# Full-height score products, and GpSimd taken off SBUF arithmetic from the output projection on

## The chip, the cores and the metric

The kernel is one launch on one core of a Trainium2 chip. The core has a matrix engine (TensorE, PE in the profile; its weight loads are listed apart as PEld), a vector engine (VectorE, DVE), a scalar engine (ScalarE, ACT), GpSimd (POOL) and SyncE (SP), which here issues most of the DMA transfers. The metric is the device time of one execution in microseconds. Before the change the median of three runs is 1672.14 us (1669.34 to 1674.14).

## The reference

One layer of a hybrid decoder, for a prompt of 1024 tokens and for 8 sequences with 4 new tokens each, 1056 columns in all, all in float32. Cut to what matters here:

```
h = rmsnorm(x) * (1 + scale1) + shift1;   z = h @ w_in + b_in      # q, k, v, forget gate, GLU, two gates
prompt:  s = q k^T / 8 + C_i - C_j, masked;  o = softmax(s) v      # 8 heads of 64, 1024 x 1024
sample:  the same against a paged cache of 1024 keys
y_b = depthwise convolution, layernorm, silu, @ w_pb + b_pb;  y_a = o @ w_pa
m = sigmoid(gate_a) * y_a + sigmoid(gate_b) * y_b
x = x + g1 * (m @ w_o)                                             # output projection, 1024 x 1024
h2 = rmsnorm(x) * (1 + scale2) + shift2
x = x + g2 * ((silu(h2 @ Wg) * (h2 @ Wu)) @ w_ffn_out)             # feed-forward, 2816 hidden
y = rmsnorm(x)
```

## The kernel before, in words

Activations lie with channels on the 128 partitions and tokens along the free axis. To come near float32 with the fast matrix format, each operand is split in a high part (a rounded copy, made on ScalarE) and a low part (operand minus high part, made on VectorE or GpSimd), and a product is three products: high times high, high times low, low times high.

The stages, in order: modulation vectors (`ada`), input projection, values, decode attention, the convolution branch (`glu`), and from about 410 us the prompt attention, with the gates' projections and the rest of `ada` filling in. Then the two branch projections (`branch`), the output projection with `w_o` (L1068 to L1092, in three column blocks c of 352 tokens), the feed-forward's first half (`hidden`, 22 tiles t), and its second half (`out`).

**Prompt attention.** A unit is a head h and a pair of query blocks c2; `softmax_rows` makes one block's scores in chunks of up to 512 keys. For each chunk TensorE runs two products into one PSUM tile: L813 over all 128 rows, and L816. The tile `q` of a head holds q's high part (negated) in one half of the partitions and the low part in the other, `k` holds the high part of k in both halves, so L813 gives high times high plus low times high. `kl` holds the low part of k in one half, and L816 takes only those 64 rows: high times low. On a diagonal chunk a third product, L815, adds the mask between them. There are 96 chunks. VectorE adds the forget term and finds the minimum (L818), ScalarE takes the exponential (L824), VectorE or ScalarE scales (L829, L827), TensorE transposes (L871), ScalarE and VectorE split the result (L873, L874), and TensorE multiplies by v (L883, L884). Two units are kept waiting between scores and `weighted`. `load_head` (L834) fetches a head's tiles about one head ahead.

**Feed-forward.** The first half runs products over blocks with a seven-product scheme: `pair_weights` (L1128) reads two weight tiles, forms sums and differences of their halves and splits seven operands (`split`, L1120); `half_factors` (L993) does the same for the activations of one half q of the tokens (`modulated` L1004, `split_u` L1018, sums L1030 to L1040). Half 0 is prepared while `w_o` still works on the last block, half 1 after tile t = 2 has begun; tiles 0 to 3 run first for half 0 alone, and for half 1 at the end.

**The order of the work.** The program is written in one order, and a list scheduler with a time model of its own places instructions on each engine; `high_priority` moves a piece ahead. Each engine then works its own list strictly in that order, so an instruction that waits holds all that stand behind it. From `w_o` on GpSimd carries: the weight split for every second tile of the last `w_o` block (L1074 to L315), L1030 and L1033 and the `split_u` of two operands in `half_factors`, and the four sums of `pair_weights` for t = 1, 2, 3 when one half alone runs.

Of the kernel before, what the change touches and what calls it, by code (L numbers as in the profile page):

```python
# [9 lines left out]
F32 = mybir.dt.float32  # L10
# [3 lines left out]
OP = mybir.AluOpType  # L14
# [15 lines left out]
KD = D // P  # L30
# [57 lines left out]
def hybrid_step(ctx, tc, xT, cT, vec, bvf, con, stT, ptab, ptabr, kcT, vc, lfc, w_ada, w_in, w_vfa, w_vfb,  # L88
                w_pa, w_pb, w_o, w_fi, w_fo, yT, kT, vO, vsO, lfO, ucp, ucs):
    nc = tc.nc  # L90
    pe, act, dve, pool, sp = nc.tensor, nc.scalar, nc.vector, nc.gpsimd, nc.sync
# [323 lines left out]
    for i, w in enumerate(first):  # L415
        ps = ps_mm()
# [4 lines left out]
        b = sm.tile([P, 1], F32, name="bsh", tag="bsh", bufs=4)  # L421
# [118 lines left out]
    for half, (src, w0, nw) in enumerate(((w_vfa, 0, 256), (w_vfb, 256, 264))):  # L540
# [261 lines left out]

    def softmax_rows(h, i, t, ck, q, k, kl):

        sl = slice(64 * (h % 2), 64 * (h % 2) + 64)
        n = P * (i + 1)
        m = sm.tile([P, 4], F32, name="mx", tag="mx", bufs=6)
        prev = 3e38
        qb = slice(i * P, (i + 1) * P)
        for nm, s0 in enumerate(range(0, n, 512)):  # L810
            w = min(512, n - s0)
            ps = ps_s()
            pe.matmul(ps[:, :w], q[:, qb], k[:, s0:s0 + w], start=True, stop=False)  # L813
            if s0 + w == n:
                pe.matmul(ps[:, w - P:w], identr, maskr, start=False, stop=False)  # L815
            pe.matmul(ps[:, :w], q[sl, qb], kl[sl, s0:s0 + w], start=False, stop=True)  # L816

            dve.tensor_tensor_reduce(out=t[:, s0:s0 + w], in0=ps[:, :w], in1=ck[:, s0:s0 + w], scale=1.0, scalar=prev,  # L818
                                     op0=OP.add, op1=OP.min, accum_out=m[:, nm:nm + 1])
            prev = m[:, nm:nm + 1]  # L820
        cq = Cq[:, i, h:h + 1]
        st = sm.tile([P, 4], F32, name="st", tag="st", bufs=6)
        dve.scalar_tensor_tensor(st[:, 1:2], prev, cq, cq, op0=OP.subtract, op1=OP.add)
        act.activation(t[:, :n], t[:, :n], AF.Exp, bias=st[:, 1:2], scale=-1.0, accum_out=st[:, 2:3])  # L824
        dve.reciprocal(st[:, 3:4], st[:, 2:3])
# [8 lines left out]
    def load_head(h):  # L834

        p, h2 = divmod(h, 2)
        qd, kd = qkD[p]
        sl = slice(64 * h2, 64 * h2 + 64)

        def head_tile(name, dt=F32R):  # L840
            return atl.tile([P, NP], dt, name=name, tag=f"{name}{h2}", bufs=1)

        q, k, kl = head_tile("q2"), head_tile("k2"), head_tile("kl")
        ck, vh = head_tile("ck", F32), head_tile("vh").rearrange("p (b n) -> p b n", n=P)
        for r in range(2):
            sp.dma_start(q[64 * r:64 * r + 64, :].bitcast(F32), qd[r ^ h2][sl, :])
            sp.dma_start(k[64 * r:64 * r + 64, :].bitcast(F32), kd[0][sl, :])
        sp.dma_start(kl[sl, :].bitcast(F32), kd[1][sl, :])
        sp.dma_start(ck, cD[h:h + 1, :].broadcast_to([P, NP]))
        sp.dma_start(vh.bitcast(F32), vD[p][:, :, h2, :])  # L850
        heads[h] = (q, k, kl, ck, vh)
# [141 lines left out]
    def half_factors(q, new):  # L993

        o = q * SUP
        if q:
            ms = ev(uq, "ms", 1, (P, KD, DB, DT))
            msf = ms.rearrange("p k b t -> p k (b t)")
            for k in range(KD):
                dve.tensor_tensor(msf[:, k, :], X(k)[:, NP:], R[:, NP:], OP.mult)  # L1000
            dve.tensor_tensor(ms, ms, gS[:, 1, :, :].unsqueeze(3).broadcast_to([P, KD, DB, DT]), OP.mult)
            dve.tensor_tensor(ms, ms, mod[:, 24:24 + KD, 1:9].unsqueeze(3).broadcast_to([P, KD, DB, DT]), OP.add)

        def modulated(i, half):  # L1004
# [12 lines left out]

        def split_u(b, k, u, eng=dve):  # L1018
            act.copy(b[0][:, k, :], u[:, k, :])
            eng.tensor_tensor(b[1][:, k, :], u[:, k, :], b[0][:, k, :].bitcast(F32), OP.subtract)  # L1020

        ks = [slice(KS * k, KS * k + KS) for k in range(4 // KS)]
        u11, u21, u12, u22 = [modulated(i, half) for half in range(2) for i in range(2)]
        b11, b21, t1, t2, b22, t3, t4 = bs = new()
        for k in ks:
            split_u(b11, k, u11)
        for k in ks:
            split_u(b21, k, u21)
        for k in ks:
            pool.tensor_tensor(u11[:, k, :], u12[:, k, :], u11[:, k, :], OP.subtract)  # L1030
            split_u(t1, k, u11)
        for k in ks:
            pool.tensor_tensor(u12[:, k, :], u22[:, k, :], u12[:, k, :], OP.subtract)  # L1033
            split_u(b22, k, u22, pool)
            dve.tensor_tensor(u22[:, k, :], u22[:, k, :], u11[:, k, :], OP.subtract)
            split_u(t2, k, u22)
        for k in ks:
            split_u(t3, k, u12, pool)
        for k in ks:
            dve.tensor_tensor(u21[:, k, :], u21[:, k, :], u22[:, k, :], OP.subtract)  # L1040
            split_u(t4, k, u21)
        return bs
# [25 lines left out]
    for c in range(3):  # L1068
        o = CW3 * c
        s = sm.tile([P, 400], F32, name="s1", tag="ssum", bufs=2)  # L1070
        for j in range(KD):

            where = () if c == 0 and j < 2 else (lt2, ("wh3", "wl3"), 3)
            w = split_ahead(w_o[j], KD, pool if c == 2 and j % 2 else dve, *where)  # L1074
            xr = ev(lt2, "xr", 3)
            for ch, (co, cn) in enumerate(CH):
                lo, hi = max(o, co), min(o + CW3, co + cn)
                if lo < hi:
                    at = KD * co + j * cn - co
# [45 lines left out]
        dve.tensor_tensor(w[:, 1, :n], raw, w[:, 0, :n].bitcast(F32), OP.subtract)  # L1125
        return w

    def pair_weights(t, eng):  # L1128

        g, u = [raw_tile(w_fi[r * HT + t], KD * P) for r in range(2)]  # L1130
        a11, a12, a21, a22 = g[:, :512], g[:, 512:], u[:, :512], u[:, 512:]
        ws = [split(a11), split(a12)]
        s1 = ev(fb or uq, "s1", 2 if fb else 1, (P, 512))
        eng.tensor_tensor(s1, a21, a22, OP.add)  # L1134
        ws.append(split(s1))
        eng.tensor_tensor(a21, a11, a21, OP.subtract)
# [262 lines left out]
```

## Time and profile before

| | |
|---|---|
| median of 3 runs | 1672.14 us |
| profiled execution | 1673.01 us, span 1671.2 us from first to last instruction |
| PE busy (matmul) | 1600.6 us, 96% |
| PEld busy (weight load) | 1486.8 us, 89% |
| DVE busy | 1074.1 us, 64% |
| ACT busy | 702.6 us, 42% |
| POOL busy | 251.9 us, 15% |
| mean granted TensorE clock | 0.980 of full speed |

The span and the execution's own time differ by 1.8 us, spent before the first and after the last instruction. TensorE is the engine that is nearly always occupied, but a busy matmul record includes the time in which it waits inside the engine; whether the weight loads run without gaps tells more. The mean share hides the stages: PEld is at its full share in most of them and lower in the prompt attention and in a stretch around 900 to 1000 us, and these two are what the tables of stretches are to be read for.

### The profile page before, as it was taken

The page shows a single profiled execution, that of the slowest core. Times are in us where ns is not written, and L with a number is a line of the kernel's source. Part 1 is how long each engine was busy: PE and PEld are TensorE (multiplying, and loading weights), DVE is VectorE, ACT ScalarE, POOL GpSimd, SP SyncE. Part 2 cuts the span into 40 slices and gives each one's busy share as a digit, 9 for nine tenths or more (in the row PEclk, how much of TensorE's full clock was granted, in tenths as well). Part 3 has the DMA queues.
Part 4 walks back from the last instruction along what each step waited for, and adds up shares of the span by engine and source line. Part 5 has one row for each costly group of instructions (what it writes and reads, how often), then busy time and mean ns, then how long its engine had stood idle before and what let it go on. Part 6 is the DMA issues. An engine that isn't in the chain of part 4 may idle for free.

```text
span 1671.2 us, 29144 instructions
## 1 busy us (share of the span) xinstructions
PE 1600.6 (96%) x10988; PEld 1486.8 (89%) x10988; DVE 1074.1 (64%) x2119; ACT 702.6 (42%) x1395; POOL 251.9 (15%) x185
## 2 busy tenths in 40 slices
PE   6999999999999999999999789999999999999997
PEld 4999978788867777989998779999999999999997
DVE  6943389999787757234678995555555587324654
ACT  4552212122476555434554554333333365324442
POOL 2121113332220001125305430000000030000000
PEclk9999999999999979999999899999999999999998
DMA  9186576877486654354674322222222246424552
GB/s 363 62 285 185 159 226 176 249 234 224 150 247 211 185 166 145 114 187 123 211 219 156 102 85 101 77 77 77 77 82 83 80 155 214 157 87 146 172 184 84
DMA packets 143087, 263.93 MB, mean 158 GB/s; under 512 B 26810, under 2 KB 84794, under 8 KB 142306
## 3 DMA queue, kind: packets, MB, share of 16 engines
q1 hardware_dynamic: 104466, 211.46, 40.6%
q10 hardware_dynamic: 36384, 43.01, 7.4%
q0 software_dynamic: 2096, 7.60, 1.5%
q8 instruction: 86, 1.41, 0.4%
q14 instruction: 55, 0.45, 0.1%
HBM read 208.54 MB, written 53.48 MB: 157 GB/s over the span
## 4 chain that ended last, share of the span: by engine, by line
PE 70%; DVE 14%; DMA 7%; issue 3%; ACT 3%; SPq 2%; POOL 1%; ACTq 0%; DVEq 0%; POOLq 0%
PE mm L1167 23%; PE mm L1268 15%; DVE acc L525 7%; PE mm L326 6%; PE mm L324 6%; PE mm L325 6%; PE ptr L871 2%; PE pss L816 2%; DMA wa<-w_ada 1%; DMA gev<-gD 1%; PE ppv L884 1%; DVE wc L1125 1%; PE mm L162 1%; PE ppv L883 1%; PE pss L813 1%
## 5 line engine op out<-in xcount | busy, mean ns | idle before, releaser
L324 PE MATMUL mm<-ah,wh 128*128 128x384 f32 (+2 forms) x768 | 254.2, 332 | 7.4 <-ACT ah L288 3.6
L1268 PE MATMUL mm<-f,wo 128*128 128x352 f32 x1584 | 256.7, 323 | 0.0
L1268 PEld LDWEIGHTS mm<-f,wo 128*128 128x128 f32 x1584 | 254.7, 188 | 0.0
L326 PE MATMUL mm<-ah,wl 128*128 128x384 f32 (+2 forms) x768 | 253.0, 331 | 1.5 <-POOL wl L315 1.5
L325 PE MATMUL mm<-al,wh 128*128 128x384 f32 (+2 forms) x768 | 254.2, 331 | 0.0
L1167 PE MATMUL mm<-b,wc 128*128 128x264 f32 x1680 | 229.6, 288 | 10.3 <-ACT gev L1172 6.9
L1167 PE MATMUL mm<-c,wc 128*128 128x264 f32 x1776 | 235.5, 286 | 3.3 <-DVE gev L1189 3.3
L1167 PEld LDWEIGHTS mm<-c,wc 128*128 128x128 f32 x1776 | 225.2, 189 | 3.7 <-DVE gev L1189 3.7
L1167 PEld LDWEIGHTS mm<-b,wc 128*128 128x128 f32 x1680 | 217.0, 191 | 11.7 <-ACT gev L1172 7.3
L315 POOL TENSOR_TENSOR wl<-wr,wh 128x1024 fp32r<-128x1024 f32 (+1 forms) x48 | 122.1, 2547 | 440.3 <-ACT wh L312 417.3
L525 DVE SCALAR_TENSOR_TENSOR acc<-u,vec,acc 128x1024 f32<-128x1024 f32 x120 | 174.1, 1472 | 1.2
L324 PEld LDWEIGHTS mm<-ah,wh 128*128 128x128 f32 x768 | 146.5, 191 | 19.2 <-issue 7.9
L325 PEld LDWEIGHTS mm<-al,wh 128*128 128x128 f32 x768 | 146.6, 191 | 12.2 <-issue 11.7
L326 PEld LDWEIGHTS mm<-ah,wl 128*128 128x128 f32 x768 | 146.4, 191 | 7.6 <-issue 4.9
L1219 DVE TENSOR_TENSOR wo<-wr,wo 128x512 fp32r<-128x512 f32 x108 | 69.7, 647 | 129.7 <-ACT wo L1218 129.1
L1124 ACT CAST wc<-wr 128x512 fp32r<-128x512 f32 x144 | 88.0, 620 | 131.2 <-PE mm L1167 123.9
L1125 DVE TENSOR_TENSOR wc<-wr,wc 128x512 fp32r<-128x512 f32 x144 | 108.6, 760 | 37.1 <-ACT wc L1124 36.0
L1218 ACT CAST wo<-wr 128x512 fp32r<-128x512 f32 x108 | 63.2, 585 | 150.3 <-PE mm L1268 145.4
L312 ACT CAST wh<-wr 128x1024 fp32r<-128x1024 f32 (+1 forms) x72 | 68.1, 951 | 91.3 <-PE mm L325 71.9
L1134 POOL TENSOR_TENSOR s<-wr 128x512 f32<-128x512 f32 x6 | 13.1, 2188 | 400.6 <-DMA wr<-w_fi 387.1
L326 PE MATMUL mm<-yh,wl 128*128 128x352 f32 x192 | 61.9, 325 | 1.2 <-POOL wl L315 1.2
L324 PE MATMUL mm<-b,wh 128*128 128x352 f32 x192 | 62.1, 323 | 0.8 <-ACT wh L312 0.8
(299 smaller groups left out, 2731.6 us busy)
## 6 DMA issues: line engine op xcount, KB each, us to landing
wr<-w_fi SPq DMA_DIRECT2D x52, 512.0 KB
wa<-w_ada SPq DMA_DIRECT2D x48, 512.0 KB
wr<-w_fo SPq DMA_DIRECT2D x36, 512.0 KB
kt<-kcT SPq DMA_DIRECT2D x64, 256.0 KB
vt<-vc SPq DMA_DIRECT2D x64, 256.0 KB
wr<-w_o SPq DMA_DIRECT2D x24, 512.0 KB
hD<-h ACTq DMA_DIRECT2D x44, 264.0 KB
wr<-w_in SPq DMA_DIRECT2D x18, 512.0 KB
```

The source lines that it names most:

```text
L312: d = act.copy(wh[:, r, :], raw[:, r, :])
L315: eng.tensor_tensor(wl[:, r, :], raw[:, r, :], wh[:, r, :].bitcast(F32), OP.subtract)
L324: pe.matmul(ps[:, :n], wh[:, k, :], xh, start=(k == 0), stop=False)
L325: pe.matmul(ps[:, :n], wh[:, k, :], xl, start=False, stop=False)
L326: pe.matmul(ps[:, :n], wl[:, k, :], xh, start=False, stop=(k == nk - 1))
L525: dve.scalar_tensor_tensor(a[:, :NP], u[:, j:j + NP], wv[:, j:j + 1], a[:, :NP], op0=OP.mult, op1=OP.add)
L1124: act.copy(w[:, 0, :n], raw)
L1125: dve.tensor_tensor(w[:, 1, :n], raw, w[:, 0, :n].bitcast(F32), OP.subtract)
L1167: pe.matmul(ps[:, :HS], w[i][:, r, k * P:(k + 1) * P], x[s][:, k, :], start=(new and k == 0 and j == 0), stop=(k == 3 and j == 2), skip_gr ...
L1218: act.copy(x[:, 0, :], raw)
L1219: dve.tensor_tensor(x[:, 1, :], raw, x[:, 0, :].bitcast(F32), OP.subtract)
L1268: pe.matmul(ps[e][:, :n], w[r][:, k * P:(k + 1) * P], f[x], start=(k0 + k + i == 0), stop=(k0 + k == HT - 1 and i == 2))
```

## The change

Two parts. In the prompt attention both halves of `q` are now laid out the same way for every head (high part first), `kl` is loaded into both halves, and L816 multiplies all 128 rows: high times low plus low times low. One more 64-row transfer of 256 KB per head is issued for it. From the output projection on, every elementwise operation that GpSimd carried goes to VectorE: 44 instructions, namely 4 weight splits of 128x1024, 8 differences and 8 splits of 128x528 in `half_factors`, and 24 sums and differences of 128x512 in `pair_weights`.

```
@@ -46,7 +46,6 @@
 KS = 2
 NHR = 8
 HF = 2
-DV = (0,)
 UW = KL + NP + DB * (KL + DT)
 
 
@@ -802,7 +801,6 @@
 
     def softmax_rows(h, i, t, ck, q, k, kl):
 
-        sl = slice(64 * (h % 2), 64 * (h % 2) + 64)
         n = P * (i + 1)
         m = sm.tile([P, 4], F32, name="mx", tag="mx", bufs=6)
         prev = 3e38
@@ -813,7 +811,7 @@
             pe.matmul(ps[:, :w], q[:, qb], k[:, s0:s0 + w], start=True, stop=False)
             if s0 + w == n:
                 pe.matmul(ps[:, w - P:w], identr, maskr, start=False, stop=False)
-            pe.matmul(ps[:, :w], q[sl, qb], kl[sl, s0:s0 + w], start=False, stop=True)
+            pe.matmul(ps[:, :w], q[:, qb], kl[:, s0:s0 + w], start=False, stop=True)
 
             dve.tensor_tensor_reduce(out=t[:, s0:s0 + w], in0=ps[:, :w], in1=ck[:, s0:s0 + w], scale=1.0, scalar=prev,
                                      op0=OP.add, op1=OP.min, accum_out=m[:, nm:nm + 1])
@@ -843,9 +841,10 @@
         q, k, kl = head_tile("q2"), head_tile("k2"), head_tile("kl")
         ck, vh = head_tile("ck", F32), head_tile("vh").rearrange("p (b n) -> p b n", n=P)
         for r in range(2):
-            sp.dma_start(q[64 * r:64 * r + 64, :].bitcast(F32), qd[r ^ h2][sl, :])
-            sp.dma_start(k[64 * r:64 * r + 64, :].bitcast(F32), kd[0][sl, :])
-        sp.dma_start(kl[sl, :].bitcast(F32), kd[1][sl, :])
+            rows = slice(64 * r, 64 * r + 64)
+            sp.dma_start(q[rows, :].bitcast(F32), qd[r][sl, :])
+            sp.dma_start(k[rows, :].bitcast(F32), kd[0][sl, :])
+            sp.dma_start(kl[rows, :].bitcast(F32), kd[1][sl, :])
         sp.dma_start(ck, cD[h:h + 1, :].broadcast_to([P, NP]))
         sp.dma_start(vh.bitcast(F32), vD[p][:, :, h2, :])
         heads[h] = (q, k, kl, ck, vh)
@@ -1015,9 +1014,9 @@
                 act.copy(u[:, :, n:], msf[:, 4 * i:4 * i + 4, :])
             return u
 
-        def split_u(b, k, u, eng=dve):
+        def split_u(b, k, u):
             act.copy(b[0][:, k, :], u[:, k, :])
-            eng.tensor_tensor(b[1][:, k, :], u[:, k, :], b[0][:, k, :].bitcast(F32), OP.subtract)
+            dve.tensor_tensor(b[1][:, k, :], u[:, k, :], b[0][:, k, :].bitcast(F32), OP.subtract)
 
         ks = [slice(KS * k, KS * k + KS) for k in range(4 // KS)]
         u11, u21, u12, u22 = [modulated(i, half) for half in range(2) for i in range(2)]
@@ -1027,15 +1026,15 @@
         for k in ks:
             split_u(b21, k, u21)
         for k in ks:
-            pool.tensor_tensor(u11[:, k, :], u12[:, k, :], u11[:, k, :], OP.subtract)
+            dve.tensor_tensor(u11[:, k, :], u12[:, k, :], u11[:, k, :], OP.subtract)
             split_u(t1, k, u11)
         for k in ks:
-            pool.tensor_tensor(u12[:, k, :], u22[:, k, :], u12[:, k, :], OP.subtract)
-            split_u(b22, k, u22, pool)
+            dve.tensor_tensor(u12[:, k, :], u22[:, k, :], u12[:, k, :], OP.subtract)
+            split_u(b22, k, u22)
             dve.tensor_tensor(u22[:, k, :], u22[:, k, :], u11[:, k, :], OP.subtract)
             split_u(t2, k, u22)
         for k in ks:
-            split_u(t3, k, u12, pool)
+            split_u(t3, k, u12)
         for k in ks:
             dve.tensor_tensor(u21[:, k, :], u21[:, k, :], u22[:, k, :], OP.subtract)
             split_u(t4, k, u21)
@@ -1071,7 +1070,7 @@
         for j in range(KD):
 
             where = () if c == 0 and j < 2 else (lt2, ("wh3", "wl3"), 3)
-            w = split_ahead(w_o[j], KD, pool if c == 2 and j % 2 else dve, *where)
+            w = split_ahead(w_o[j], KD, dve, *where)
             xr = ev(lt2, "xr", 3)
             for ch, (co, cn) in enumerate(CH):
                 lo, hi = max(o, co), min(o + CW3, co + cn)
@@ -1125,18 +1124,18 @@
         dve.tensor_tensor(w[:, 1, :n], raw, w[:, 0, :n].bitcast(F32), OP.subtract)
         return w
 
-    def pair_weights(t, eng):
+    def pair_weights(t):
 
         g, u = [raw_tile(w_fi[r * HT + t], KD * P) for r in range(2)]
         a11, a12, a21, a22 = g[:, :512], g[:, 512:], u[:, :512], u[:, 512:]
         ws = [split(a11), split(a12)]
         s1 = ev(fb or uq, "s1", 2 if fb else 1, (P, 512))
-        eng.tensor_tensor(s1, a21, a22, OP.add)
+        dve.tensor_tensor(s1, a21, a22, OP.add)
         ws.append(split(s1))
-        eng.tensor_tensor(a21, a11, a21, OP.subtract)
-        eng.tensor_tensor(a11, s1, a11, OP.subtract)
+        dve.tensor_tensor(a21, a11, a21, OP.subtract)
+        dve.tensor_tensor(a11, s1, a11, OP.subtract)
         ws.append(split(a11))
-        eng.tensor_tensor(a12, a12, a11, OP.subtract)
+        dve.tensor_tensor(a12, a12, a11, OP.subtract)
         ws.append(split(a12))
         ws.append(split(a21))
         ws.append(split(a22))
@@ -1152,7 +1151,7 @@
 
 
         with tc.high_priority(offset=OW if len(halves) == 2 else ON):
-            w = pair_weights(t, dve if len(halves) == 2 or t in DV else pool)
+            w = pair_weights(t)
         for q in halves:
             hidden_half(t, q, w)
```

The scheduler places the program anew. On the list of SyncE, a head's loads before (the tiles `qkD` are the parts of q and k in memory; L846 and L847 fill the two halves of q and k, L848 fills one half of kl):

```order
L846 DMA q_5252<-qkD_387 64x1024
L847 DMA k_5253<-qkD_389 64x1024
L846 DMA q_5252<-qkD_388 64x1024
L847 DMA k_5253<-qkD_389 64x1024
L848 DMA kl<-qkD_390 64x1024
L849 DMA ck<-cD 128x1024
L850 DMA vh<-vD_1043 128x8x128
```

and now (line numbers are one lower from here on):

```order
L845 DMA q_5252<-qkD_387 64x1024
L846 DMA k_5253<-qkD_389 64x1024
L847 DMA kl<-qkD_390 64x1024
L845 DMA q_5252<-qkD_388 64x1024
L846 DMA k_5253<-qkD_389 64x1024
L847 DMA kl<-qkD_390 64x1024
L848 DMA ck<-cD 128x1024
L849 DMA vh<-vD_1043 128x8x128
```

A second load of kl stands among them, and all the loads come in pairs of halves.

On the list of VectorE, where the first tile of the feed-forward is prepared (`wc` are split weights, `XA`, `XB` the residual stream, `u` the modulated activations, `b` their split parts, `s` a weight sum), before:

```order
L315 TENSOR_TENSOR wl<-wr,wh 128x1024
L1125 TENSOR_TENSOR wc<-wr,wc 128x512
L1051 SCALAR_TENSOR_TENSOR XB<-mm,mod,xr 128x320
L1125 TENSOR_TENSOR wc<-wr,wc 128x512
L1058 TENSOR_TENSOR XA<-xr,rs 128x32
L1055 TENSOR_TENSOR rs<-mm,mod 128x32
L1020 TENSOR_TENSOR b<-u,b 128x528
L1058 TENSOR_TENSOR XB<-xr,rs 128x32
L1051 SCALAR_TENSOR_TENSOR XB<-mm,mod,xr 128x320
L1055 TENSOR_TENSOR rs<-mm,mod 128x32
L1020 TENSOR_TENSOR b<-u,b 128x528
L1134 TENSOR_TENSOR s_11032<-wr 128x512
```

and now:

```order
L314 TENSOR_TENSOR wl<-wr,wh 128x1024
L1029 TENSOR_TENSOR u<-u 128x528
L1124 TENSOR_TENSOR wc<-wr,wc 128x512 x2
L1050 SCALAR_TENSOR_TENSOR XB<-mm,mod,xr 128x320
L1029 TENSOR_TENSOR u<-u 128x528
L1057 TENSOR_TENSOR XA<-xr,rs 128x32
L1054 TENSOR_TENSOR rs<-mm,mod 128x32
L1032 TENSOR_TENSOR u<-u 128x528
L314 TENSOR_TENSOR wl<-wr,wh 128x1024
L1019 TENSOR_TENSOR b<-u,b 128x528
L1050 SCALAR_TENSOR_TENSOR XB<-mm,mod,xr 128x320
L1019 TENSOR_TENSOR b<-u,b 128x528
```

The differences `u<-u` (L1029 and L1032 now) and a second weight split `wl` have come in between, and the later entries stand so much further down.

On the list of GpSimd, before, from the end of the branch projection on (`wl` a low part of a weight, `gev` a sum of the two branches, `rv` a constant):

```order
L315 TENSOR_TENSOR wl<-wr,wh 128x512
L965 TENSOR_TENSOR gev<-gev,XB 128x352 x3
L192 MEMSET rv 128x4
L315 TENSOR_TENSOR wl<-wr,wh 128x1024 x2
L192 MEMSET rv 128x4
L315 TENSOR_TENSOR wl<-wr,wh 128x1024
L1030 TENSOR_TENSOR u<-u 128x528 x2
L1033 TENSOR_TENSOR u<-u 128x528 x2
L315 TENSOR_TENSOR wl<-wr,wh 128x1024
L1020 TENSOR_TENSOR b<-u,b 128x528 x4
L1134 TENSOR_TENSOR s_11150<-wr 128x512
L1136 TENSOR_TENSOR wr<-wr 128x512
```

and now, to the end of the program:

```order
L964 TENSOR_TENSOR gev<-gev,XB 128x352 x3
L314 TENSOR_TENSOR wl<-wr,wh 128x512
L964 TENSOR_TENSOR gev<-gev,XB 128x352 x3
L191 MEMSET rv 128x4 x4
L1394 UNCONDITIONAL_BRANCH
```

Only small memsets are left.

## Rows read from the trace of the kernel before

**Rows 1.** Busy time by stretch, all engines; columns are named in the first row.
```profile
core 0: us, PE busy (x) PEld busy (x) DVE busy (x) ACT busy (x) POOL busy (x), PEclk, DMA share, GB/s
440.00:560.00 120.00, 118.31 (x757) 90.54 (x755) 96.25 (x322) 78.47 (x162) 19.07 (x20) 1.00 0.67 198
560.00:671.00 111.00, 108.37 (x672) 82.32 (x671) 70.23 (x218) 61.74 (x127) 7.15 (x3) 0.92 0.53 159
895.00:990.00 95.00, 74.45 (x507) 71.97 (x505) 93.13 (x152) 55.01 (x116) 49.88 (x30) 0.89 0.27 89
1000.00:1320.00 320.00, 320.00 (x2623) 320.00 (x2623) 175.98 (x333) 124.46 (x268) 0.00 (x0) 1.00 0.24 82
1320.00:1400.00 80.00, 76.74 (x608) 76.32 (x608) 58.47 (x100) 42.65 (x96) 17.61 (x12) 0.98 0.43 138
```

**Rows 2.** Waits of PE from 410 to 671: us in total, times, longest.
```profile
PE mm L162 <- DMA wa<-w_ada: 3.3, 2, 2.6
PE ppv L884 <- DVE ptl L874: 0.8, 1, 0.8
```

**Rows 3.** The same two stretches, instructions of L816 alone; columns PE, PEld, clock, DMA.
```profile
440.00:560.00 120.00, 21.03 (x48) 8.77 (x48) 1.00 0.67 198
560.00:671.00 111.00, 19.55 (x42) 8.29 (x42) 0.92 0.53 159
```

**Rows 4.** Weight loads in order of time: start us, us, instruction, idle before.
```profile
522.09 0.19 PEld L813 LDWEIGHTS pss<-k,q 128*128 128x128 f32 x1
522.51 0.18 PEld L816 LDWEIGHTS pss<-kl,q 64*128 64x128 f32 x1 [0.24 <-issue]
522.94 0.19 PEld L813 LDWEIGHTS pss<-k,q 128*128 128x128 f32 x1 [0.25 <-issue]
523.05 0.19 PEld L815 LDWEIGHTS pss<-maskr,identr 128*128 128x128 f32 x1
523.43 0.18 PEld L816 LDWEIGHTS pss<-kl,q 64*128 64x128 f32 x1 [0.19 <-issue]
523.86 0.19 PEld L883 LDWEIGHTS ppv<-pth,vh 128*128 128x128 f32 x1 [0.25 <-ACT py L824]
523.97 0.19 PEld L884 LDWEIGHTS ppv<-ptl,vh 128*128 128x128 f32 x1
```

**Rows 5.** DVE groups, 895 to 990: count, busy us, mean ns, idle before.
```profile
L1125 DVE TENSOR_TENSOR wc<-wr,wc 128x512 fp32r<-128x512 f32 x19 | 19.8, 1051 | 0.0
L1125 DVE TENSOR_TENSOR b<-wr,b 128x512 fp32r<-128x512 f32 x9 | 8.8, 982 | 0.7 <-ACT b L1124 0.7
L1011 DVE SCALAR_TENSOR_TENSOR u<-XB,gP,R 128x264 f32<-128x264 f32 x8 | 5.5, 753 | 0.0
L1125 DVE TENSOR_TENSOR wc<-s,wc 128x512 fp32r<-128x512 f32 x3 | 4.1, 1367 | 0.0
L1190 DVE TENSOR_TENSOR h<-gev 128x264 f32<-128x264 f32 x3 | 3.5, 1151 | 0.0
L1011 DVE SCALAR_TENSOR_TENSOR u<-XA,gP,R 128x264 f32<-128x264 f32 x8 | 3.4, 489 | 0.4 <-ACT R L1090 0.4
L211 DVE SCALAR_TENSOR_TENSOR ry<-rt,ry 128x3 f32<-128x3 f32 x3 | 2.6, 860 | 0.1
L210 DVE SCALAR_TENSOR_TENSOR rt<-rt,rv 128x3 f32<-128x3 f32 x3 | 0.5, 162 | 0.1
```

**Rows 6.** The same view of the quiet stretch 1000 to 1320.
```profile
L1125 DVE TENSOR_TENSOR wc<-wr,wc 128x512 fp32r<-128x512 f32 x93 | 63.9, 690 | 33.0 <-ACT wc L1124 32.1
L1190 DVE TENSOR_TENSOR h<-gev 128x264 f32<-128x264 f32 x31 | 13.4, 434 | 2.9 <-ACT wc L1124 0.4
```

**Rows 7.** One subtraction on both engines (L1020): duration ns min/median/max.
```profile
L1020 DVE TENSOR_TENSOR b<-u,b x10: 693/698/1784, 867.8 to 926.5; 128x528 fp32r<-128x528 f32 x10
L1020 POOL TENSOR_TENSOR b<-u,b x4: 1299/1546/1769, 906.5 to 917.3; 128x528 fp32r<-128x528 f32 x4
```

**Rows 8.** Waits of PE from 1320 to 1400.
```profile
PE mm L1167 <- DVE gev L1189: 3.3, 2, 2.5
```

More of the change, by code (lines that the diff above doesn't have):

```diff
@@ L48 @@
 HF = 2
-DV = (0,)
 UW = KL + NP + DB * (KL + DT)
@@ L803, in softmax_rows @@
     def softmax_rows(h, i, t, ck, q, k, kl):
-        sl = slice(64 * (h % 2), 64 * (h % 2) + 64)
         n = P * (i + 1)
@@ L815, in softmax_rows @@
                 pe.matmul(ps[:, w - P:w], identr, maskr, start=False, stop=False)
-            pe.matmul(ps[:, :w], q[sl, qb], kl[sl, s0:s0 + w], start=False, stop=True)
+            pe.matmul(ps[:, :w], q[:, qb], kl[:, s0:s0 + w], start=False, stop=True)
             dve.tensor_tensor_reduce(out=t[:, s0:s0 + w], in0=ps[:, :w], in1=ck[:, s0:s0 + w], scale=1.0, scalar=prev,
@@ L845, in load_head @@
         for r in range(2):
-            sp.dma_start(q[64 * r:64 * r + 64, :].bitcast(F32), qd[r ^ h2][sl, :])
-            sp.dma_start(k[64 * r:64 * r + 64, :].bitcast(F32), kd[0][sl, :])
-        sp.dma_start(kl[sl, :].bitcast(F32), kd[1][sl, :])
+            rows = slice(64 * r, 64 * r + 64)
+            sp.dma_start(q[rows, :].bitcast(F32), qd[r][sl, :])
+            sp.dma_start(k[rows, :].bitcast(F32), kd[0][sl, :])
+            sp.dma_start(kl[rows, :].bitcast(F32), kd[1][sl, :])
         sp.dma_start(ck, cD[h:h + 1, :].broadcast_to([P, NP]))
@@ L1016, in modulated, with split_u @@
             return u
-        def split_u(b, k, u, eng=dve):
+        def split_u(b, k, u):
             act.copy(b[0][:, k, :], u[:, k, :])
-            eng.tensor_tensor(b[1][:, k, :], u[:, k, :], b[0][:, k, :].bitcast(F32), OP.subtract)
+            dve.tensor_tensor(b[1][:, k, :], u[:, k, :], b[0][:, k, :].bitcast(F32), OP.subtract)
         ks = [slice(KS * k, KS * k + KS) for k in range(4 // KS)]
@@ L1029, in half_factors @@
         for k in ks:
-            pool.tensor_tensor(u11[:, k, :], u12[:, k, :], u11[:, k, :], OP.subtract)
+            dve.tensor_tensor(u11[:, k, :], u12[:, k, :], u11[:, k, :], OP.subtract)
             split_u(t1, k, u11)
         for k in ks:
-            pool.tensor_tensor(u12[:, k, :], u22[:, k, :], u12[:, k, :], OP.subtract)
-            split_u(b22, k, u22, pool)
+            dve.tensor_tensor(u12[:, k, :], u22[:, k, :], u12[:, k, :], OP.subtract)
+            split_u(b22, k, u22)
             dve.tensor_tensor(u22[:, k, :], u22[:, k, :], u11[:, k, :], OP.subtract)
@@ L1037, in half_factors @@
         for k in ks:
-            split_u(t3, k, u12, pool)
+            split_u(t3, k, u12)
         for k in ks:
@@ L1073, in hybrid_step @@
             where = () if c == 0 and j < 2 else (lt2, ("wh3", "wl3"), 3)
-            w = split_ahead(w_o[j], KD, pool if c == 2 and j % 2 else dve, *where)
+            w = split_ahead(w_o[j], KD, dve, *where)
             xr = ev(lt2, "xr", 3)
@@ L1126, in split, with pair_weights @@
         return w
-    def pair_weights(t, eng):
+    def pair_weights(t):
         g, u = [raw_tile(w_fi[r * HT + t], KD * P) for r in range(2)]
@@ L1133, in pair_weights @@
         s1 = ev(fb or uq, "s1", 2 if fb else 1, (P, 512))
-        eng.tensor_tensor(s1, a21, a22, OP.add)
+        dve.tensor_tensor(s1, a21, a22, OP.add)
         ws.append(split(s1))
-        eng.tensor_tensor(a21, a11, a21, OP.subtract)
-        eng.tensor_tensor(a11, s1, a11, OP.subtract)
+        dve.tensor_tensor(a21, a11, a21, OP.subtract)
+        dve.tensor_tensor(a11, s1, a11, OP.subtract)
         ws.append(split(a11))
-        eng.tensor_tensor(a12, a12, a11, OP.subtract)
+        dve.tensor_tensor(a12, a12, a11, OP.subtract)
         ws.append(split(a12))
@@ L1154, in hidden @@
         with tc.high_priority(offset=OW if len(halves) == 2 else ON):
-            w = pair_weights(t, dve if len(halves) == 2 or t in DV else pool)
+            w = pair_weights(t)
         for q in halves:
```

## The prediction

> **What bounds the kernel now.** Read the busy shares first, then the same by stretch, then what TensorE waits for, then its weight loads. TensorE's matmul records cover 96% of the span, which says little, since a record also covers waiting inside the engine. The stretches say more [rows 1]. From 1000 to 1320 matmul and weight load are both busy for all 320 us: nothing but the number of products sets the pace there, and 2623 products of 264 columns in 320 us are 0.122 us each, 0.46 ns per column. Two kinds of stretch fall short of that.
>
> The first is the prompt attention. PE is recorded busy for 118.3 of 120 us and 108.4 of 111 us, yet the weight loads fill only 90.5 and 82.3 us [rows 1]. TensorE hardly waits for another engine there: 3.3 us for weights by DMA and 0.8 us for VectorE are the longest waits of 261 us [rows 2]. So the missing time is lost inside TensorE, and the weight loads in order of time show where [rows 4]. A product whose successor has the same shape lets the next load start early: after L813 the load for L815 comes 0.11 us later, and L884's follows L883's at 0.11 us. Around L816, the only product that takes 64 rows, it is otherwise: its load stands 0.24 us idle before it, and so does the load after it (0.25 us). Both wait until the product before has left the array.
>
> The second is 895 to 990 us, where the last block of the output projection runs into the feed-forward. PE is busy for only 74.5 of 95 us at a granted clock of 0.89 of full speed (a part of the time at 1.2 GHz instead of 2.4), while DVE is busy for 93.1 us [rows 1]. VectorE sets the pace. Its instructions there take far longer than the same ones in the quiet stretch: 1051 against 690 ns, 1151 against 434 ns [rows 5, 6]. GpSimd is busy for 49.9 us of those 95 and for none of the 320 quiet ones [rows 1], and the longest of a subtraction on VectorE, 1784 ns against a median of 698, is as long as one GpSimd instruction (1299 to 1769 ns) on top of it or nearly so [rows 7]. I read it thus: a VectorE instruction with both operands in SBUF is held until the GpSimd instruction beside it has ended.
>
> **The change part by part.** I sum against the profiled execution, 1673.0 us (span 1671.2 and 1.8 outside); that is 0.9 us above the median of 1672.1.
>
> *Full-height L816.* From the load of one L813 to that of the next, 522.09 to 522.94, 0.85 us pass for two products of 512 columns, which at 0.46 ns per column want 0.47: 0.38 us lost. From 522.94 to the load of L883 at 523.86, 0.92 us pass for 512 + 128 + 512 columns, which want 0.53: 0.39 lost [rows 1, 4]. So each L816 costs about 0.38 us in its two neighbourhoods. There are 48 and 42 of them in the two stretches [rows 3], that is 18.2 and 16.0 us, 34 us in all; this is the ceiling. With 128 rows L816 has the shape of its neighbours, and both waits should go. The product itself streams the same columns.
>
> What is late next? In the first stretch, 120 - 18 = 102 us would hold 96.3 us of VectorE work [rows 1], 94%. A chain in which VectorE answers TensorE and is answered by it does not run at that. The only stretch where VectorE is fuller is the one at 895, where PE stands. I let VectorE reach 90%, so 107 us: 13 us gained, with 0 and 18 as ends. In the second, 111 - 16 = 95 us would hold 70.2 us of VectorE (74%) and 61.7 of ScalarE (65%) [rows 1], which hide. But the weights that `ada` waits for come by DMA, whose wait of 3.3 us [rows 2] cannot shrink and may grow as the work around it gets shorter: I take 2 us off and keep 14 of 16. Together 27 us, ends 0 and 34.
>
> The additional transfer is 256 KB for each head on SyncE's queue, eight in all. At 198 GB/s, the mean of the first stretch at a DMA share of 0.67 [rows 1], it is 1.3 us each, loaded about one head ahead of its use; I cost it at nothing. If that cover is gone, all eight cost 10 us.
>
> *GpSimd's work on VectorE, 895 to 990.* Of GpSimd's 30 instructions in this stretch [rows 1], 28 are sums, differences or splits of 512 or 528 columns, one is a weight split of 1024 and one a memset. On an unhindered VectorE they take about 0.69 us each (698 ns median [rows 7], 690 [rows 6]); the wide one about twice that. So 28 x 0.69 + 1.4 = 20.7 us are added. What is given back is the time held. By the groups shown [rows 5], against quiet durations [rows 6] or the same operation unheld in this stretch (489 ns for 753, 162 for 860 [rows 5]): 19 x 0.361 + 9 x 0.292 + 3 x 0.677 (`wc`, `b`, `wc` of a sum) = 11.5; 8 x 0.264 = 2.1; 3 x 0.717 = 2.2; 3 x 0.698 = 2.1. That is 17.9 us from five groups that hold 42 of the 152 instructions. Further groups, each with an instruction or two held, make it more; the ceiling is GpSimd's own 49.9 us less its memset. I take 28, so VectorE's work falls by about 7 us, and where VectorE paces, the stretch gets shorter by as much. A little comes back beside it: sums that took 1.3 us and more on GpSimd now stand 0.69 us ahead of the splits that need them, and fewer pauses mean less time at 1.2 GHz. I take 8 us. The ends: 20.5 us gained (all of PE's idle time) and 20.7 lost (nothing given back).
>
> The Trainium skill speaks against this part: its page Perfetto Trace Analysis, section Optimizing Scalar/DVE Operations, says that with a saturated vector engine moving work off to GpSimd may make sense, and adds that the two share a read port of SBUF, so that it might not help. By the first half of that the change would cost the 20.7 us. The trace here bears out the second half: 17.9 us and more of held time stand against it.
>
> *The same before 895 and after 1320.* Three of the four weight splits of the last `w_o` block run before 895, where PE is at its full share; what VectorE takes there is hidden. From 1320 to 1400 the 12 sums for the last tiles move: 12 x 0.69 = 8.3 us more on VectorE, whose load is 58.5 of 80, against GpSimd's 17.6 us in which it may be held [rows 1]. PE waits 3.3 us there for VectorE [rows 8]. I take 1.5 us gained; ends 3.3 gained, 8.3 lost.
>
> Sum: 27 + 8 + 1.5 = 36.5. 1673.0 - 36.5 = 1636.5, and 0.9 less against the median: 1636.
>
> **The rivals.**
> *A. VectorE and the loads take back most of the attention's gain.* For it: 96.3 us of VectorE in the first stretch, a DMA share of 0.67, a wait for `wa` that is already the longest [rows 1, 2]; and the granted clock, already 0.92 in the second stretch, where that wait lies, would fall further with longer ones. Against it: TensorE waits almost nowhere now. Then the first stretch gives 4 us and the second 8: 1673 - 12 - 9.5 - 0.9, about 1651.
>
> *B. The gaps are not due to the 64 rows.* They might belong to three products into one PSUM tile. Against it: L815 goes into the same tile as L813 with a gap-free load [rows 4]. Then the attention stays, and only 9.5 us come: 1663.
> The Trainium skill has a rule that points this way: TensorE: Matmul & The Clock Gate, section Why this matters for your kernels, puts one product over 32 rows at the time of one over 128, by which full height would gain nothing. The trace shows 0.38 us lost beside each product over 64 rows; that the rule is about a product among its like, and not about a change of shape, no run here shows.
>
> *C. Slower: VectorE is full and nothing is given back.* If the long VectorE instructions of 895 to 990 are slow for another reason than GpSimd, the 20.7 us and the 8.3 us land on the pacing engine, 29 us. PE then stands 20.7 us longer, with more of its 507 products at half clock: if the half-clock share doubles from about 0.22 (clock 0.89) to 0.44, that is 0.22 x 507 x 0.122 = 14 us. It decides when less than about 10 of the 29 us come back: 1673 + 29 + 14 - 27 - 0.9 = 1688. For it: DVE at 93.1 of 95. Against it: the holding is seen in five different instructions, and never in the quiet stretch.
>
> **How the numbers follow.** Forecast 0.66 (1617 to 1645), A 0.18, B 0.07, C 0.05; 0.04 is left for a mix of C and the forecast that ends within 0.3% (5 us), about what a measurement of this kernel can tell from no change. Faster: the forecast, A, and B (9.5 us are 0.6%), nearly all: 0.90. Within: 0.04 and a little of B, 0.05. Slower: 0.05. The low end of the range is 34 + 16 (four fifths of PE's idle time from 895 to 990) + 3 us of gain, 1619, and 2 more for a clock that falls less often; the high end takes in A and stops before B: 1659.
>
> **What would show it.** Right: weight loads of the second product follow without idle time; PEld's busy share in the attention rises towards that of 1000 to 1320; the last L884 ends 22 to 34 us earlier; from then to about 860 the distance stays; around 900 to 990 VectorE's split is at about 690 ns throughout, and PE is full some 8 us earlier. Wrong: idle time before L816's successor as before (B); PE waits for L818, L829 or `wa` in the attention of more than 15 us (A); VectorE instructions still at 1000 ns and more beside an empty GpSimd (C).

## The result and the profile after

The changed kernel takes 1630.97 us in the median of four runs (1629.62 to 1633.62), the kernel before beside it 1672.95 (1669.34 to 1674.14): a ratio of 0.9755, 95% interval 0.9735 to 0.9774, 41 us less. 1636 was predicted, 1617 to 1659 as its range. The same changed kernel was timed again in a later series (below, e7): 1636.6 against 1666.6, ratio 0.9829 (0.9805 to 0.9854), some 30 us less. The two series differ by more than either interval says, so the parts are weighed by the length of stages inside each trace.

The stages are cut at six marks that every variant has: the first score product, the last product with v (L884 before), the copy of the second block's scale to `R` (L1090), the eighth product into `h` (L1194), the sixth from last of these, and the last.

| us | to first score | attention | to `R` | feed-forward starts | its middle | its end | rest |
|---|---|---|---|---|---|---|---|
| before | 410.4 | 287.4 | 196.5 | 135.1 | 317.0 | 56.0 | 268.8 |
| after | 407.6 | 263.9 | 193.9 | 124.3 | 317.5 | 52.7 | 269.4 |
| e7 (after again) | 411.6 | 266.8 | 194.4 | 123.5 | 316.9 | 53.6 | 269.2 |
| e1 scores only | 410.9 | 262.1 | 193.1 | 135.7 | 316.8 | 57.5 | 268.8 |
| e2 GpSimd only | 409.5 | 286.2 | 196.0 | 125.1 | 315.1 | 53.5 | 268.8 |
| e8 (e2 again) | 406.0 | 285.6 | 195.9 | 125.0 | 315.2 | 54.1 | 268.8 |
| e3 idle GpSimd work | 408.9 | 265.9 | 193.7 | 138.3 | 316.6 | 55.9 | 268.8 |
| e4 pair sums on GpSimd | 405.4 | 263.2 | 194.4 | 130.9 | 315.1 | 55.9 | 268.8 |
| e5 no GpSimd at all | 413.7 | 277.1 | 190.2 | 124.4 | 317.2 | 53.5 | 268.8 |
| e6 splits on VectorE | 414.9 | 267.2 | 190.8 | 122.9 | 317.0 | 53.1 | 269.1 |

The profiled execution is 41.9 us shorter than that of before, by its marks: attention 23.5, start of the feed-forward 10.8, its end 3.3, the stretch to `R` 2.6, and 2.8 ahead of the first score product, where nothing was changed; the remaining stages give 1.1 back. The first column is 405.4 to 411.6 us in eight profiles whose code is alike up to there, so a few us of any total are not the edit's. The two shortest, 405.4 in e4 and 406.0 in e8, had a granted clock of 0.97 and 1.00 of full speed in the first 100 us, the other six 0.94 or 0.95.

The mark between the feed-forward's start and its middle does not always stand behind the same number of products: e2, e4 and e8 have 841 or 842 in the start, the others of these eight 825 to 832. All have 3425 in the two stages together, so the two are best added: 452.1 us before, 441.8 after, 440.5 in e7, 440.3 in e2 and in e8, 452.5 in e1, 454.9 in e3, 446.0 in e4.

The weight loads of a diagonal chunk, after (columns as in [rows 4]):

```profile
499.99 0.14 PEld L870 LDWEIGHTS ptr<-con,py 128*128 128x128 f32 x1
500.10 0.19 PEld L811 LDWEIGHTS pss<-k,q 128*128 128x128 f32 x1
500.21 0.19 PEld L813 LDWEIGHTS pss<-maskr,identr 128*128 128x128 f32 x1
500.33 0.19 PEld L814 LDWEIGHTS pss<-kl,q 128*128 128x128 f32 x1
500.46 0.45 PEld L870 LDWEIGHTS ptr<-con,px 128*128 128x128 f32 x4
```

L814 is what L816 was. No idle time stands at it or behind it; in [rows 4] it was 0.19 to 0.25 us on each side. Over all 96 chunks, idle time of more than 0.1 us stood before 66 of the loads of L816 and behind 81; after, it stands before 1 of those of L814 and behind 22.

The same stretches by engine, after; those from the feed-forward on are shifted by 30 to 40 us against [rows 1]:

```profile
core 0: us, PE busy (x) PEld busy (x) DVE busy (x) ACT busy (x) POOL busy (x), PEclk, DMA share, GB/s
440.00:560.00 120.00, 113.69 (x828) 96.81 (x826) 101.66 (x341) 85.42 (x174) 18.42 (x20) 0.99 0.73 213
560.00:671.00 111.00, 104.93 (x761) 92.21 (x759) 68.46 (x208) 64.37 (x135) 10.82 (x5) 0.97 0.59 174
865.00:960.00 95.00, 82.78 (x586) 80.46 (x586) 90.91 (x198) 60.64 (x125) 0.10 (x1) 0.93 0.32 106
1280.00:1360.00 80.00, 78.78 (x633) 78.14 (x632) 58.26 (x115) 43.74 (x98) 0.00 (x0) 1.00 0.44 143
```

In the attention 828 products stand where 757 stood, and 761 where 672 stood, while PE itself is busy for less time: it now waits for others. Its longest waits there, beside [rows 2]:

```profile
PE mm L161 <- DMA wa<-w_ada: 5.7, 5, 2.0
PE ptr L870 <- DVE ptl L873: 5.3, 4, 2.0
PE pst L776 <- DVE lnsum L774: 1.8, 1, 1.8
```

Those for weights have grown from 3.3 to 5.7 us, those for the split of the probabilities from 0.8 to 5.3. At the start of the feed-forward VectorE is as full as before (90.9 of 95 us), but with 198 instructions instead of 152. Each takes its quiet time, beside [rows 5] and [rows 6]:

```profile
L1124 DVE TENSOR_TENSOR wc<-wr,wc 128x512 fp32r<-128x512 f32 x22 | 14.6, 690 | 0.0
L1124 DVE TENSOR_TENSOR b<-wr,b 128x512 fp32r<-128x512 f32 x10 | 6.9, 690 | 2.3 <-ACT b L1123 2.2
L1010 DVE SCALAR_TENSOR_TENSOR u<-XB,gP,R 128x264 f32<-128x264 f32 x8 | 3.4, 486 | 0.0
L1189 DVE TENSOR_TENSOR h<-gev 128x264 f32<-128x264 f32 x5 | 2.1, 428 | 0.0
L210 DVE SCALAR_TENSOR_TENSOR ry<-rt,ry 128x3 f32<-128x3 f32 x3 | 0.5, 156 | 0.0
```

### The profile page after: what moved, and what is told of

Read it like the earlier page. It is cut to its first block, busy times and chain, and to the rows that moved or that the text cites. A ratio compares the mean times of both kernels' runs of the same rounds, so it can differ in the third digit from the quotient of the medians.

```text
span 1629.3 us, 29106 instructions
## 1 busy us (share of the span) xinstructions
PE 1562.8 (96%) x10988; PEld 1477.1 (91%) x10988; DVE 1054.7 (65%) x2163; ACT 704.6 (43%) x1397; POOL 176.0 (11%) x141
## 4 chain that ended last, share of the span: by engine, by line
PE 60%; DVE 9%; DMA 5%; ACT 1%; issue 1%; POOL 1%; SPq 0%; ACTq 0%; DVEq 0%; POOLq 0%
PE mm L1166 24%; PE mm L1267 15%; PE mm L325 5%; PE mm L324 5%; PE mm L323 5%; DVE acc L524 2%; PE ptr L870 1%; DMA wa<-w_ada 1%; PE ppv L883 1%; PE mm L161 1%; PE ppv L882 1%; DMA sq<-hD 1%; DVE wc L1124 1%; PE pss L814 1%; PE pss L811 1%
## 5 line engine op out<-in xcount | busy, mean ns | idle before, releaser
L314 POOL TENSOR_TENSOR wl<-wr,wh 128x1024 fp32r<-128x1024 f32 (+1 forms) x44 | 110.4, 2512 | 394.1 <-ACT wh L311 331.5
L1124 DVE TENSOR_TENSOR wc<-wr,wc 128x512 fp32r<-128x512 f32 x144 | 98.2, 690 | 36.3 <-ACT wc L1123 35.3
L324 PE MATMUL mm<-yl,wh 128*128 128x352 f32 x192 | 62.0, 324 | 0.1
```

Of the source, the lines that this page charges most:

```text
L314: eng.tensor_tensor(wl[:, r, :], raw[:, r, :], wh[:, r, :].bitcast(F32), OP.subtract)
L324: pe.matmul(ps[:, :n], wh[:, k, :], xl, start=False, stop=False)
```

## The experiments

**e1, the attention part alone.** The diff of the change in `softmax_rows` and `load_head`, and nothing else.

> The attention part alone: 128-row second product and the second load of kl, GpSimd's work as before the change. Theory (each change of shape between 128 and 64 rows cost TensorE a wait, and the attention was paced by TensorE): 26 us off, 1647 us (1641 to 1652), the last product with v some 26 us earlier, the stretch from the output projection on as long as before. Rival (the 42 us came mainly from the feed-forward, where the pacing engine got free): no more than 10 us off, 1663 or above.

Measured: 1646.3 us (1644.4 to 1647.1), ratio 0.9867 (0.9845 to 0.9890). The attention is 25.3 us shorter, the feed-forward's start as before (135.7 against 135.1, or 452.5 against 452.1 with the middle). The theory holds.

**e2 and e8, GpSimd's part alone.** The rest of the diff.

> GpSimd's work on VectorE alone, attention as before the change. Theory (VectorE was held by GpSimd for longer than the moved work takes): 14 us off, 1659 us (1655 to 1663): about 11 around the start of the feed-forward and 3 near its end. Rival (VectorE is full there, the moved work adds about 20 us, and the gain of the whole change came from the attention alone): 1673 or slower.

> The part that takes GpSimd off alone, a second look: its first profile was of one of its two slowest runs (1656, the other four 1645 to 1648). If the nine us between them lie in the attention or before it, they are no part of what the edit does (the attention again 286 us); if they lie from 890 us on, the theory's 14 us are too few.

Measured: 1647.0 us (1645.3 to 1656.0), ratio 0.9877 (0.9852 to 0.9902), more than expected; e8 took 1652.6 (one run). In both profiles the attention is as before within 1.8 us, and the feed-forward gives 11.8 us in its start and middle (10.0 or 10.1 by the mark of the start alone) and 2.5 or 1.9 at its end, as expected. What e8 has over e2 is 3.5 us ahead of the attention. The kernel before, on that chip, ran from 1660 to 1673 us. The medians of the parts do not add up: e1 is 22.5 us and e2 21.8 us faster than the kernel before, both parts together (e7) only 29.9. No profile fell on one of e2's four runs at 1645 to 1648 us; their mean granted clock is 0.987 to 0.989, that of the profiled run at 1656 us 0.981. Where they saved more stays open.

**e3, GpSimd busy for nobody.**

```
             dve.tensor_tensor(b[1][:, k, :], u[:, k, :], b[0][:, k, :].bitcast(F32), OP.subtract)
+            pool.tensor_tensor(idle, b[0][:, k, :200].bitcast(F32), b[1][:, k, :200].bitcast(F32), OP.add)
```

> The changed kernel, and beside each of the 28 splits of half_factors GpSimd adds two SBUF tiles (400 columns) into a tile that nobody reads: 28 instructions of about 1.1 us, no work for VectorE. Theory (a VectorE instruction with two SBUF operands is held while GpSimd runs one): VectorE's instructions near them grow from 0.69 us to up to 1.8, up to 30 us held, and the kernel loses 10 to 25 us: 1641 to 1656. Rival (the feed-forward gained because the sums are ready sooner on the faster engine, not because VectorE was held): 1631, as the changed kernel.

Measured: 1649.9 us (1643.7 to 1651.3), ratio 0.9881. The feed-forward's start takes 138.3 us instead of 124.3, longer than before the change, though VectorE has the same work as in the changed kernel. Its weight splits, and GpSimd's additions, from 868 to 967 us:

```profile
L1126 DVE TENSOR_TENSOR wc<-wr,wc 128x512 fp32r<-128x512 f32 x19 | 16.0, 858 | 0.0
```
```profile
L1020 POOL TENSOR_TENSOR idle<-b 128x400 f32<-128x400 f32 x10 | 14.5, 1445 | 27.9 <-DVE rs L1056 18.6 <-DVE b L1019 6.9 <-DVE XB L1059 1.9
L1020 POOL TENSOR_TENSOR idle<-c 128x400 f32<-128x400 f32 x8 | 14.4, 1795 | 31.9 <-DVE c L1019 31.6
```

The same splits take 858 ns on average instead of 690: held by work that only occupies GpSimd. No instruction waited for GpSimd's results. The theory of the held engine stands, that of the sooner sums falls. The end of the feed-forward also lost its 3 us (55.9), with no idle work near: TensorE waits 2.5 us for ScalarE's `gev` there, against 0.8 after, and the granted clock is 0.97 instead of 1.00. Why `gev` comes late is not shown; the scheduler placed that part anew, too.

**e4, the sums of pair_weights on GpSimd again.** `pair_weights` gets back its argument, `dve if len(halves) == 2 or t == 0 else pool`, for its four sums.

> The changed kernel with the sums of pair_weights for t = 1, 2, 3 on GpSimd again where one half alone runs (24 instructions, 12 at the start of the feed-forward and 12 near its end); the differences and splits of half_factors stay on VectorE. Theory (time held against time added): at the start 12 x 1.4 us held against 12 x 0.69 saved, so about 8 us lost, and 2 to 3 near the end: 1640 us (1636 to 1645). Rival (only half_factors counted, the sums are off the pacing chain): 1631 to 1633.

Measured: 1641.2 us (1635.9 to 1642.7). The start takes 130.9 us, but with 842 products instead of 825; with the middle, 446.0 us against 441.8 (440.5 in e7): 4.2 lost of 10.3, or 5.5 of 11.6, so the sums make up somewhat less than half of the gain there. The end takes 55.9 us, 3.2 lost, all of it; the wait of [rows 8] is back, 3.2 us.

**m1, both mechanisms by themselves.** Behind the last product of the changed kernel, in short (W is 128x128, M and N 128x512):

```
+    def full(i):        pe.matmul(acc[0], W, M)                      # a
+    def half(i):        pe.matmul(acc[0], W[:64, :], M[:64, :])      # b
+    def in_turn(i):     half(i) if i % 2 else full(i)                # c
+    def both_halves(i): lower, then upper 64 rows of W and M         # d
+    def columns(i):     W[:, :32] if i % 2 else W                    # e
...
+    two_sbuf: dve.tensor_tensor(d, a, N)   one_psum: dve.tensor_tensor(d, a, acc[0])
+    one_sbuf: dve.tensor_scalar(d, a, 2.0) beside:   pool.tensor_tensor(g, a, N)
```

> The changed kernel with two measurements added behind its last product; its time is some 60 us longer for them. TensorE: blocks of 24 products of 512 columns each, (a) all 128 rows, (b) all the lower 64 rows, (c) 128 and 64 rows in turn, (d) lower and upper 64 rows in turn, (a) again, (e) 128 and 32 stationary columns in turn. Theory (a change of shape lets the array run empty, 64 rows by themselves are harmless): (a) and (b) 0.21 to 0.24 us each product, (c) 0.40 to 0.44, (e) as (c), (d) as (b) or faster. Rival (a product over 64 rows is slow in itself): (b) as slow as (c) or slower. VectorE: eight subtractions of 512 columns alone, then beside GpSimd's additions: with two SBUF operands, with one SBUF and one PSUM operand, with one SBUF operand alone. Theory (held only where both operands are in SBUF): 0.69 us alone, 1.2 to 2 us with two SBUF operands beside GpSimd, undisturbed (0.55 to 0.7) with an operand in PSUM. Rival (any VectorE work is slowed by GpSimd): all three slower.

Its time, 1730.0 us, is 93 longer than e7's, not 60: TensorE's part takes 37 us of it, VectorE's and GpSimd's 55. The weight loads, in order of time (L1334 is a, L1337 b, L1343 and L1341 c, L1347 d, L1353 and L1351 e):

```profile
1640.03 5.33 PEld L1337 LDWEIGHTS mm<-M,W 64*128 64x128 f32 x24 [0.35 <-issue]
1645.71 0.19 PEld L1343 LDWEIGHTS mm<-M,W 128*128 128x128 f32 x1 [0.35 <-issue]
1646.14 0.18 PEld L1341 LDWEIGHTS mm<-M,W 64*128 64x128 f32 x1 [0.24 <-issue]
...
1655.58 0.18 PEld L1341 LDWEIGHTS mm<-M,W 64*128 64x128 f32 x1 [0.25 <-issue]
1655.59 2.81 PEld L1347 LDWEIGHTS mm<-M,W 64*128 64x128 f32 x24
1658.75 5.31 PEld L1334 LDWEIGHTS mm<-M,W 128*128 128x128 f32 x24 [0.35 <-issue]
1664.10 0.19 PEld L1353 LDWEIGHTS mm<-M,W 128*128 128x128 f32 x1
1664.33 0.11 PEld L1351 LDWEIGHTS mm<-M,W 128*32 128x32 f32 x1
1664.55 0.19 PEld L1353 LDWEIGHTS mm<-M,W 128*128 128x128 f32 x1
```

24 loads fill 5.33 us over 64 rows and 5.31 over 128: 0.22 us a product, alike. (The first block of a, before these rows, took 6.68 us, at a granted clock of 0.79; the others ran at 1.00.) In turn they stand 0.43 apart, with 0.24 us idle at each. So the change of row count costs, not the row count: rival B and the slow product both fall. Lower and upper halves in turn run at 0.12 us. Where I was wrong is (e): 128 and 32 stationary columns in turn follow at 0.23 us, without idle time.

VectorE and GpSimd, eight instructions of 512 columns to a row:

```profile
1671.33 5.78 DVE L1369 TENSOR_TENSOR md<-ma,N 128x512 f32<-128x512 f32 x8 [39.70 <-ACT ma L1361]
1677.84 12.37 DVE L1369 TENSOR_TENSOR md<-ma,N 128x512 f32<-128x512 f32 x8 [0.74 <-ACT ma L1361]
1692.01 5.74 DVE L1372 TENSOR_TENSOR md<-ma,mm 128x512 f32<-128x512 f32 x8 [1.80 <-ACT ma L1361]
1703.40 10.23 DVE L1375 TENSOR_SCALAR md<-ma 128x512 f32<-128x512 f32 x8 [5.65 <-ACT ma L1361]
```
```profile
1677.89 13.44 POOL L1378 TENSOR_TENSOR mg<-ma,N 128x512 f32<-128x512 f32 x8 [150.71 <-ACT ma L1361]
1692.06 10.67 POOL L1378 TENSOR_TENSOR mg<-ma,N 128x512 f32<-128x512 f32 x8 [0.73 <-ACT ma L1361]
1715.48 10.64 POOL L1378 TENSOR_TENSOR mg<-ma,N 128x512 f32<-128x512 f32 x8 [0.73 <-ACT ma L1361]
```

With two SBUF operands VectorE takes 0.72 us alone and 1.55 beside GpSimd, whose own work grows from 10.64 to 13.44 us: they run in turn, one of each every 1.67 us. With one operand in PSUM neither notices the other (5.74, 10.67). The product `a * 2.0`, with a single SBUF operand, takes 1.28 us beside GpSimd; I had expected it undisturbed. It was not timed alone, but the first of its eight began before GpSimd did and lasted 0.43 us, the other seven 1.37 each. Sixteen operations shared between the two want 13.4 us, and VectorE alone would do all sixteen in 11.6 (an estimate, 16 times 0.72).

**e5, e6, e7: farther down that road.** e6 moves the weight splits of the convolution branch and the gates to VectorE (`w_in_tile(12 + ct, dve, pool)`, `gate(i, dve, sp)` and so on); e5 moves also the first stage's, the layernorm's and the branches'. e7 is the changed kernel on their chip.

> The changed kernel with all elementwise work of GpSimd on VectorE from the first stage on (weight splits of the input projection, the gates and the branches, the layernorm's sums, the merged branches); only memsets, two kinds of small copies and its DMA issues stay. Theory (beside GpSimd's 176 us VectorE is held for some 58 us, 22 of them where the convolution fills VectorE from 200 to 407 us; the same work takes VectorE about 1.23 us per split of 1024 columns, about 75 us in all): where VectorE paces (200 to 430) 22 given back against 17 added, 3 to 6 us gained; a little in the attention; nothing from 671 to 865, where TensorE is full: 1622 to 1630 where the changed kernel has 1631. Rival (VectorE, now near full in the attention too, becomes the bound): 1635 or slower.

> The changed kernel with the weight splits of the convolution branch and the gates on VectorE (200 to 671 us); the first stage, the layernorm and the branches stay as they are. Theory: 3 to 6 us gained in the convolution stretch and 0 to 4 in the attention, 1622 to 1629. Rival as before: 1635 or slower.

> The changed kernel once more, on the chip of e5 and e6, so that these two are compared with it there: 1631 (1628 to 1634) by both theories.

Measured: e5 1646.6 us (1642.9 to 1648.2), e6 1636.8 (1632.9 to 1639.7), e7 1636.6 (1634.4 to 1639.2). e6 gains nothing, and e5 loses 10: the theory fails there. It had the hold right: the convolution's steps, in e7 and in e6 (ns min/median/max):

```profile
L524 DVE SCALAR_TENSOR_TENSOR acc<-u,vec,acc x120: 1248/1280/3416, 223.9 to 425.6; 128x1024 f32<-128x1024 f32 x120
```
```profile
L524 DVE SCALAR_TENSOR_TENSOR acc<-u,vec,acc x120: 1246/1279/1286, 220.9 to 433.9; 128x1024 f32<-128x1024 f32 x120
```

None is held any more, yet the last starts at 433.9 instead of 425.6. VectorE works its list in order, and from 200 us to the first score product it is busy for less time in e6 (181.9 us against 191.2 in e7) but idle for more (33.0 against 20.4). Its longest waits from 200 to 415 us, in e7 and in e6:

```profile
DVE u L510 <- PE mm L325: 16.1, 3, 9.6
DVE dt L696 <- PE pss L688: 2.5, 1, 2.5
```
```profile
DVE u L510 <- PE mm L325: 12.6, 5, 3.9
DVE wl L314 <- ACT wh L311: 8.4, 4, 6.2
DVE dt L696 <- PE pss L688: 6.5, 3, 3.9
```

The 8.4 us are new: the split that GpSimd had waited for stands in VectorE's own list now, ahead of the convolution. Nor was there much to gain: TensorE, recorded idle for 6.0 of the 211.6 us from 200 to the first score product in e7, was nearly full, where the theory had VectorE pace. That these waits alone cost e6 its gain is not shown. In e5 the attention takes 277.1 us (266.8 in e7): 6.7 of the 10.3 us more are idle time of TensorE (22.4 against 15.7), the rest busy time at a granted clock of 0.95 instead of 0.97. Its longest waits there are

```profile
PE mm L161 <- DMA wa<-w_ada: 9.0, 7, 3.2
PE pss L811 <- DVE mx L816: 5.2, 2, 3.5
PE ppv L882 <- ACT pth L872: 4.0, 2, 3.8
```

The 3.6 us that e6 shows from the attention to `R` are gate products that ran earlier (1152 products in that stage against 1197, and 41 more ahead of the first score product, in a first column 3.3 us longer), no gain. No version was found that beats the changed kernel.

## Why the prediction was right, step by step

**What bounds the attention.** Right. The gaps around L816 were inside TensorE and due to the change of row count: the after profile, e1 and m1 show it one by one. 27 us were forecast of a ceiling of 34; the stage gave 23.5 (20.6 in e7, 25.3 in e1, 21.5 in e3, 24.2 in e4, 19.7 in m1). The ceiling itself came out: over all 96 chunks it was 96 x 0.38 = 36 us, and PE's busy time in the stage fell by 33.0, from 282.7 to 249.7. The term that was too small is what would be late next. PE's recorded idle time over the stage was 4.7 us (of 287.4) and is 14.2 after (of 263.9), so 9.5 us went to new waits, where the sum had left 7: 2.4 more for `wa` and 4.5 more for VectorE's split of the probabilities, and 1.5 more for the layernorm's sum (`lnsum`), by their rows. The prediction had named VectorE's work and `wa` (rival A in small). The cut at 90% of VectorE was not what happened: it is at 101.7 of 120 us, 85%. The last gap of [rows 4], 0.25 us before L883, is put down to ScalarE by its row; the prediction counted it as one of shape.

**The extra load of kl.** Costed at nothing. No wait of PE for q, k or kl is among the longest after; nothing separates a small cost from that of `wa`.

**GpSimd's work on VectorE.** Right in kind, small in size: 8 us were forecast at the start of the feed-forward, 10.3 measured with the middle (11.6 in e7, 11.8 in e2 and e8); 1.5 at its end, 3.3 measured (1.9 to 2.5 alone): there PE's wait of 3.3 us for VectorE became one of 0.8 for ScalarE and one of 0.5, and the granted clock rose from 0.97 to 1.00. The step that the sum rested on, that the long VectorE instructions were held and would go back to their quiet time, is shown by 1051 becoming 690 ns, by e3 and by m1; rival C falls. The 28 us that I took for the held time were chosen between 17.9 and 49.9, and they were right: the excess of each VectorE instruction in the stage over the median of its kind with GpSimd idle adds up to 28.4 us before, 28.3 in e1 and 0.4 after. VectorE's busy time there fell from 122.6 to 110.8 us, by 11.8 and not 7, so by these figures the moved work took it some 16.6 us, an estimate, and not 20.7: that cost was the term set too high. The held groups listed are six, with 45 instructions, and not five with 42; their sum of 17.9 stands.

**Between the stages.** The stretch from the attention to `R` was to stay and got 2.1 to 2.6 us shorter, in e1 as well (3.4) but not in e2. PE's recorded idle time there fell from 4.2 us to 2.1 after and 1.3 in e1 (3.9 in e2): its waits for GpSimd's weight split and for ScalarE's `yh` and `wh` are shorter. Why these come sooner is not shown.

**The sum.** 36.5 forecast, 41.9 between the profiles, 35.1 between that of before and e7's. That 1636 came within 5 us of 1631 owes something to chance: two gains were forecast too low, one too high, and a few us lie in a stage that the change does not touch.

## What to carry to other kernels

A stretch where PE's records are full but its weight loads are not is worth its own look: order the loads by time and see which neighbour opens the gap. A product over 64 rows among full ones cost the overlap of two weight loads here, 0.38 us, more than filling the rows with a term one may as well compute. Beside a full VectorE, GpSimd was no second pair of hands where both read two SBUF operands (13.4 us for sixteen operations, where VectorE alone wants some 11.6). But moving its work over paid only where VectorE paced TensorE; where VectorE's list then has to wait for what GpSimd waited for, as in e6, nothing came of it.

## What the runs showed of the hardware that was not expected

Products over the lower and the upper 64 rows in turn, into two PSUM tiles, followed each other at 0.12 us for 512 columns, half the time of products of one kind (0.22). Stationary tiles of 128 and 32 columns in turn cost no gap (0.23 us each), unlike 128 and 64 rows (0.43). The Trainium skill (TensorEngine Tiling (Array Packing), section Key Properties) says that a change of tiling mode drains TensorE: the rows agree for 64 rows, and for 32 columns at the tile's left edge they show no drain; whether such a product changes the mode at all, no row here shows. A VectorE product with a constant, one SBUF operand only, was slowed beside GpSimd from 0.43 us to 1.37, while a subtraction with one operand in PSUM was not slowed (0.69 us throughout, as two SBUF operands take alone). The Trainium skill (SBUF — State Buffer, section Who interferes with whom) counts such products among those that can take the port pair shared with GpSimd; the 1.37 us agree. GpSimd is slowed by VectorE as well: 1.33 us became 1.68.
